# Seven block products instead of eight in the up projections of an encoder's last three FFNs

## The chip, the cores and the metric

The kernel runs on one core of one Trainium2 chip. The metric is the device time of one execution in microseconds (us); the figure given is the median of three runs. A profile is one execution, recorded by the hardware profiler.

In the texts PE is the matrix engine, PEld its loading of the stationary operand, DVE the vector engine, ACT the scalar engine, POOL a general engine, SP the engine that issues nearly all transfers (DMA). PE adds products up in PSUM banks, from which DVE and ACT read; everything else lies in SBUF.

## The reference

A trunk of two layers over 256 tokens of 1024 channels. Each layer is a feed-forward network (FFN), a mixing sub-layer and a second FFN, so the stages are FFN, mix, FFN, FFN, mix, FFN. What matters here is the FFN:

```python
def swiglu(h, w_up, w_down):
    a, b = jnp.split(h @ w_up, 2, axis=-1)
    return (jax.nn.silu(a) * b) @ w_down
...
        h = rms_norm(x, ffn1_pre_g[l])
        x = x + 0.5 * rms_norm(swiglu(h, ffn1_w_up[l], ffn1_w_down[l]), ffn1_post_g[l])
```

`w_up` is 1024 x 5632 (gate half, value half), `w_down` 2816 x 1024, all float32.

## The kernel before, in words

**Split operands.** A float32 product is made of three matmuls: each operand is a high part (rounded to the PE's reduced float32) and a low part (the rest), and high x high, high x low and low x high are added in one bank (`mm3`). ACT casts the high part, DVE subtracts it from the original for the low part (`split` for tokens and hidden values, `next_unit` for weights).

**Weights.** They come as units of 128 x 2048 (1 MB), laid out on the host in the order of use. SP loads them into `raw` tiles (pool `rawp`, three buffers); `next_unit` splits one into `wh` and `wl` (pool `wts`, five pairs of buffers), in two halves of 1024 columns, or in four quarters for the first five units of a stage. A buffer is loaded or split anew when its last reader is done.

**An FFN.** The 2816 hidden channels are 11 pairs of 128. For each pair the up projection needs two units (gate and value columns), the down projection one. Two pairs come first; then, for pair p from 2 to 10, the up projection of p and the down unit of p - 2 (`down`, `rows_chunk`: 24 matmuls into four banks `acc` that stay open for the whole FFN); the last three down units, first all token half 0 and then all token half 1, make the tail, which ends in `post_norm` and the next stage's `pre_norm`. Tokens are two halves c of 128; `xx` holds them transposed, high and low, as eight blocks of 128 channels.

**Two forms of the up projection.** The conventional one (`form_b2`; the first FFN throughout, pairs 0 and 1 elsewhere) keeps a token block stationary and moves 512 weight columns, 24 matmuls for each token half; `swiglu` makes the product with the gate, and two PE transposes a half (`turn`, kept in `pending` until a `flush`) bring it to the hidden tile `hid`. The other (`up2`, `form_a2`; pairs 2 to 10 of the last three FFNs) keeps the weights stationary and moves all tokens, 512 columns (high and low) for the high weight and 256 for the low one, so that its result is already transposed.

**What sets the order.** Each engine works through one queue in order. A scheduler orders the queues when the program is built, from the code's order and the buffers that are free; a wait in a queue holds up everything behind it. SP's transfers wait in its queue for their buffers. `ahead()`, called after pair 4, prepares the next mix in an FFN that comes ahead of one: in the fourth stage `mem_gain`, which loads the transposed memory tokens and splits them.

Of the kernel before, what the change touches and what calls it, by code (L numbers as in the profile page):

```python
# [17 lines left out]
P = 128  # L18
# [17 lines left out]
T_SC = (242, 336)  # L36
T_KT = (200, 222)
# [10 lines left out]
def encoder_kernel(ctx, tc, x_d, xt_d, mem_d, memt_d, pos_d, w_d, gains_d, cols_d, lamv_d, poolw_d, cst_d, out_d):  # L48
# [4 lines left out]
    rawp = ctx.enter_context(tc.tile_pool(name="rawp", bufs=3))  # L53
# [17 lines left out]
    def mb_bank():  # L71
        return mmp.tile([P, 512], F32, name="mb")
# [32 lines left out]
    def next_unit():  # L105
        parts = 4 if fine[0] > 0 else 2
        fine[0] -= 1
        if not raws:
            load_unit()
        raw = raws.pop(0)  # L110
        h = wts.tile([P, 2048], F32R, name="wh")
        l = wts.tile([P, 2048], F32R, name="wl")
        n = 2048 // parts
        for s in range(parts):
            cs = slice(s * n, (s + 1) * n)
            high = nc.scalar.copy(out=h[:, cs], in_=raw[:, cs])  # L116
            low = nc.vector.tensor_tensor(out=l[:, cs], in0=raw[:, cs], in1=h.bitcast(F32)[:, cs], op=ALU.subtract)  # L117
# [4 lines left out]
        return h, l  # L122

# [55 lines left out]
    def pre_norm(c, src, g, xx):  # L179
# [24 lines left out]
        return turn  # L204
# [81 lines left out]
    def ffn(i, xx, late, g_post, finish, ahead, raw_rstd=None):  # L286
# [4 lines left out]
        def hid_pair(p):  # L291
            hid[p] = (hids.tile([P, 2, 2, P], F32R, name="hid"), hids.tile([P, 2, 2, P], F32R, name="hid"))
            return hid[p]

        def lhs_of(c, kk, k):
            return hid[kk][0][:, c, k, :], hid[kk][1][:, c, k, :]

        def down(p):
# [7 lines left out]
        pending = []  # L306

        def flush():
            while pending:
                pending.pop(0)()  # L310
# [7 lines left out]

        def up_first(p, ws):
            banks = [ma_bank(), ma_bank()]  # L320
            for i, w in enumerate(ws):
                for c in range(2):
                    mm3(banks[c], half_b(w, i, c, xx), i == 0, i == 1)
            for c in range(2):
                swiglu(p, c, banks[c])

        def swiglu(p, c, ps):
            sg = t2((P, 2, P))
            gate, value = (ps[:, 256 * j:256 * j + 256].rearrange("p (u m) -> p u m", u=2) for j in range(2))
            hn = t2((P, 2, P))  # L330
            if raw_rstd:
                nc.scalar.activation(out=sg, in_=gate, func=AF.Silu, scale=raw_rstd[c])
                nc.vector.scalar_tensor_tensor(out=hn, in0=value, scalar=raw_rstd[c], in1=sg, op0=ALU.mult, op1=ALU.mult)
            else:
                nc.scalar.activation(out=sg, in_=gate, func=AF.Silu)
                nc.vector.tensor_tensor(out=hn, in0=value, in1=sg, op=ALU.mult)

            def turn():
                tp = mb_bank()
                for u in range(2):  # L340
                    nc.tensor.transpose(out=tp[:, u * P:(u + 1) * P], in_=hn[:, u, :], identity=ident)  # L341
                tv = tp[:, 0:256].rearrange("p (u t) -> p u t", u=2)
                split(tv, hid[p][0][:, c], hid[p][1][:, c])

            pending.append(turn)

        def up2(p, u):
            w = next_unit()
            banks = [ma_bank(), mb_bank()]
            for i in range(2):  # L350
                form_a2(banks[i], w, slice(i * P, (i + 1) * P), xx)
            flush()
            t = t2()
            for i in range(2):
                half = t[:, i * S:(i + 1) * S]
                nc.scalar.copy(out=half, in_=banks[i][:, S:2 * S])  # L356
                nc.vector.tensor_tensor(out=half, in0=banks[i][:, 0:S], in1=half, op=ALU.add)  # L357
            nc.scalar.activation(out=t[:, 0:S], in_=t[:, 0:S], func=AF.Silu)  # L358
            nc.vector.tensor_tensor(out=t[:, 0:S], in0=t[:, 0:S], in1=t[:, S:2 * S], op=ALU.mult)
            split(t[:, 0:S].rearrange("p (c t) -> p c t", c=2), hid[p][0][:, :, u, :], hid[p][1][:, :, u, :])  # L360

        ws = [(next_unit(), next_unit()) for _ in range(1 if raw_rstd else 2)]
        if raw_rstd:
            hs, ls = first_high, first_low
# [6 lines left out]
        for p in range(2):  # L371
            hid_pair(p)
        if raw_rstd:
# [3 lines left out]
        else:  # L377
            done = []
# [4 lines left out]
        for p in range(2, NPR):  # L383
            hid_pair(p)
            if raw_rstd:
                w2 = (next_unit(), next_unit())
                for c in range(2):
                    up(p, c, w2)
            else:
                for u in range(2):  # L390
                    up2(p, u)
            if p - 2 <= NPR - 4:
                down(p - 2)
            if p == 4:
                ahead()
        todo = [(next_unit(), p) for p in range(NPR - 3, NPR)]
# [125 lines left out]
    def mix(l, xx, late, mm, finish):  # L522
# [10 lines left out]
        vc = mixp.tile([P, 2, S], F32, name="vc")  # L533
        up = mixp.tile([P, 2, S + 16], F32, name="up")
        pooled = mixp.tile([P, 2, S], F32, name="pooled")
        pw = mixp.tile([P, 2, P], F32, name="pw")
# [261 lines left out]

    for i, (kind, l, row) in enumerate(stages):
        nx = {}  # L800

        def finish(c):
# [5 lines left out]
            if c == 0:  # L808
                nx["xx"] = xt_pair()
                nx["g"] = gain(stages[i + 1][1] * 10 + stages[i + 1][2])  # L810
            return pre_norm(c, halves(x[c]), nx["g"], nx["xx"])()

        if kind == "ffn":
# [7 lines left out]
            late = ffn(i, cur, late, gain(l * 10 + row + 1), finish, ahead, [rst[:, c:c + 1] for c in range(2)] if i == 0 else None)  # L821
        else:
            late = mix(l, cur, late, mem, finish)
        cur, mem = nx.get("xx"), nx.get("mem")
# [24 lines left out]
def _pack(a, np):  # L849
# [5 lines left out]

    def wide(w, idx):
        both = w[:, idx].reshape(2, 4, P, 512).transpose(0, 2, 1, 3)
        units.extend(np.ascontiguousarray(both[i]).reshape(P, 2048) for i in range(2))
# [4 lines left out]
    def ffn(up, down, first):  # L863
        for p in range(NPR):
            if p < 2 or first:
                wide(up, np.r_[256 * p:256 * p + 256, D_FF + 256 * p:D_FF + 256 * p + 256])
            else:
                for i in (2 * p, 2 * p + 1):
                    cols(up, np.r_[P * i:P * i + P, D_FF + P * i:D_FF + P * i + P])
            if 0 <= p - 2 <= NPR - 4:  # L870
                rows(down, p - 2)
# [61 lines left out]
```

## Time and profile before

| | |
|---|---|
| runs shown | 1138.71 us median (1138.63 to 1139.41) |
| the profiled execution's own time | 1138.92 us |
| its span, first to last instruction | 1136.9 us |
| busy: PE, DVE, ACT | 1127.8, 749.6, 626.8 us |
| one late FFN (third stage, 384.20 to 570.05 us) | 185.85 us, DVE busy 120.77 |
| one repeat in it, an up pair and a down unit | 16.72 us |
| bytes read from HBM | 216.33 MB, mean 191 GB/s |

The profiled execution's time is 0.2 us above the median; 2.0 us lie outside its span. Lines are named L and a number. In groups by line an entry reads: line, engine, operation, output tile <- input tiles, shapes, count | busy us, mean ns of one | idle us of the engine just before them and what ended it. A chain row is a start, a length and a piece. A matmul's duration includes its way through the array, so that two in a row overlap; the distance between starts is what one costs.

### The profile page before, as it was taken

To read this page: it belongs to the slowest core of one execution; us is meant where nothing else is said; L and a number is where in the kernel's file an instruction comes from. 1 tells how busy PE (TensorE), PEld (TensorE's weight loads), DVE (VectorE), ACT (ScalarE), POOL (GpSimd) and SP (SyncE) were. 2 spreads that over 40 slices of the span, in tenths; PEclk is the share of its full clock that TensorE was granted. 3 is DMA by queue.
4 is the path that set the end of the run, shared out by engine and by line. 5 is a ranking of instruction groups with operands and counts; after the bars stand their busy time and mean duration, and the time that the engine had idled before them with its cause. 6 is when DMAs were issued, how large, how long until landed. Compare 5 with 4: busy or idle time off the path is not lost.

```text
span 1136.9 us, 14731 instructions
## 1 busy us (share of the span) xinstructions
PE 1127.8 (99%) x5679; PEld 943.7 (83%) x5679; DVE 749.6 (66%) x1164; ACT 626.8 (55%) x1121; POOL 25.6 (2%) x37
## 2 busy tenths in 40 slices
PE   9999999999999999999999999999999999999997
PEld 6888888888788888888888888888887888888886
DVE  6767456567758866566586756575676688666553
ACT  7666445456573565555565655555566546555541
POOL 0000000000000100000000000010000001000000
PEclk9999999999999999999999999999999999999999
DMA  8976553544554575555465655545455545655530
GB/s 318 340 239 229 194 189 131 213 171 148 205 183 168 204 256 192 186 185 186 148 238 206 222 189 184 186 158 204 161 180 184 203 148 177 249 185 185 186 111 37
DMA packets 35493, 218.32 MB, mean 192 GB/s; under 512 B 4192, under 2 KB 4448, under 8 KB 11232
## 3 DMA queue, kind: packets, MB, share of 16 engines
q1 hardware_dynamic: 35424, 217.40, 53.4%
q8 instruction: 44, 0.72, 0.2%
q14 instruction: 25, 0.20, 0.1%
HBM read 216.33 MB, written 1.05 MB: 191 GB/s over the span
## 4 chain that ended last, share of the span: by engine, by line
PE 97%; DMA 1%; ACT 1%; DVE 0%; POOL 0%; issue 0%; SPq 0%; DVEq 0%; POOLq 0%; ACTq 0%
PE ma L224 36%; PE acc L266 25%; PE mb L243 13%; PE ma L243 13%; PE mb L224 2%; PE acc L224 2%; PE mb L199 1%; PE acc L599 1%; PE mb L341 1%; PE acc L622 1%; PE mb L497 1%; PE acc L685 1%; DMA hid<-in_xt 1%; DMA raw<-in_w 0%; PE acc L669 0%; PE mb L758 0%
## 5 line engine op out<-in xcount | busy, mean ns | idle before, releaser
L117 DVE TENSOR_TENSOR wl<-raw,wh 128x1024 fp32r<-128x1024 f32 (+1 forms) x444 | 459.0, 1075 | 150.8 <-ACT wh L116 145.0
L116 ACT CAST wh<-raw 128x1024 fp32r<-128x1024 f32 (+1 forms) x444 | 391.3, 935 | 187.8 <-issue 99.9
L224 PE MATMUL ma<-wh,xhl 128*128 128x512 f32 x1184 | 376.6, 393 | 0.8 <-ACT wh L116 0.8
L224 PEld LDWEIGHTS ma<-wh,xhl 128*128 128x128 f32 x1184 | 221.4, 188 | 47.5 <-ACT wh L116 1.7
L224 PE MATMUL ma<-wl,xhl 128*128 128x512 f32 x592 | 233.6, 395 | 0.2 <-DVE wl L117 0.2
L266 PE MATMUL acc<-wh,hid 128*128 128x512 f32 x704 | 224.6, 391 | 0.0
L243 PE MATMUL ma<-xhl,wh 128*128 128x512 f32 x432 | 157.4, 398 | 0.0
L243 PE MATMUL mb<-xhl,wh 128*128 128x512 f32 x432 | 157.0, 397 | 0.0
L266 PEld LDWEIGHTS acc<-wh,hid 128*128 128x128 f32 x704 | 132.2, 188 | 26.2
L266 PE MATMUL acc<-wl,hid 128*128 128x512 f32 x352 | 137.1, 389 | 0.0
L224 PEld LDWEIGHTS ma<-wl,xhl 128*128 128x128 f32 x592 | 111.3, 188 | 23.9 <-DVE wl L117 1.2
L243 PE MATMUL mb<-xhl,wl 128*128 128x256 f32 x432 | 112.5, 281 | 0.0
L243 PE MATMUL ma<-xhl,wl 128*128 128x256 f32 x432 | 112.4, 281 | 0.0
L243 PEld LDWEIGHTS ma<-xhl,wh 128*128 128x128 f32 x432 | 81.2, 188 | 15.8
L243 PEld LDWEIGHTS mb<-xhl,wh 128*128 128x128 f32 x432 | 81.5, 189 | 14.5
L357 DVE TENSOR_TENSOR s<-mb,s 128x256 f32<-128x256 f32 x54 | 22.9, 424 | 103.8 <-ACT s L356 103.8
L243 PEld LDWEIGHTS mb<-xhl,wl 128*128 128x128 f32 x432 | 81.6, 189 | 5.0
L243 PEld LDWEIGHTS ma<-xhl,wl 128*128 128x128 f32 x432 | 81.5, 189 | 4.6
L266 PEld LDWEIGHTS acc<-wl,hid 128*128 128x128 f32 x352 | 66.2, 188 | 13.7
L356 ACT COPY s<-mb 128x256 f32<-128x256 f32 x54 | 20.2, 373 | 58.7 <-PE mb L243 58.7
L358 ACT ACTIVATE s<-s 128x256 f32<-128x256 f32 x54 | 22.6, 418 | 50.6 <-DVE s L357 50.6
L140 POOL TENSOR_TENSOR sm<-sm,mhalf 128x1 f32<-128x1 f32 (+1 forms) x26 | 22.6, 869 | 1024.5 <-DVE sm L149 845.6
(162 smaller groups left out, 966.0 us busy)
## 6 DMA issues: line engine op xcount, KB each, us to landing
raw<-in_w SPq DMA_DIRECT2D x189, 1024.0 KB, 4.8
gain<-in_gains SPq DMA_DIRECT2D x17, 512.0 KB, 5.1
raw<-in_w SPq DMA_DIRECT2D x8, 256.0 KB, 5.7
hid<-in_memt SPq DMA_DIRECT2D x8, 256.0 KB, 6.0
hid<-in_xt SPq DMA_DIRECT2D x4, 256.0 KB, 5.6
raw<-in_w SPq DMA_DIRECT2D x2, 512.0 KB, 6.9
x<-in_x SPq DMA_DIRECT2D x4, 256.0 KB, 6.6
hid<-in_mem SPq DMA_DIRECT2D x4, 256.0 KB, 6.1
```

The costliest lines, as they stand in the source:

```text
L116: high = nc.scalar.copy(out=h[:, cs], in_=raw[:, cs])
L117: low = nc.vector.tensor_tensor(out=l[:, cs], in0=raw[:, cs], in1=h.bitcast(F32)[:, cs], op=ALU.subtract)
L140: nc.gpsimd.tensor_tensor(out=r, in0=v, in1=mhalf[:, :n], op=ALU.pow)
L199: tps.append(nc.tensor.transpose(out=ps[:, k * P:(k + 1) * P], in_=xn[:, i * P:(i + 1) * P], identity=ident))
L224: done.append(nc.tensor.matmul(out=out, lhsT=lhsT, rhs=rhs, start=(first and i == 0), stop=(last and i == n - 1)))
L243: nc.tensor.matmul(out=o, lhsT=ww[:, k, ms], rhs=rhs, start=(k == 0 and o is full), stop=(k == KT - 1 and o is full))
L266: done.append(nc.tensor.matmul(out=banks[b], lhsT=a, rhs=ww[:, k, fs], start=(kk == first and k == 0 and i == 0), stop=(kk == last and k = ...
L341: nc.tensor.transpose(out=tp[:, u * P:(u + 1) * P], in_=hn[:, u, :], identity=ident)
L356: nc.scalar.copy(out=half, in_=banks[i][:, S:2 * S])
L357: nc.vector.tensor_tensor(out=half, in0=banks[i][:, 0:S], in1=half, op=ALU.add)
L358: nc.scalar.activation(out=t[:, 0:S], in_=t[:, 0:S], func=AF.Silu)
L497: ins.append(nc.tensor.transpose(out=tp[:, i * P:(i + 1) * P], in_=a[:, hh, kt * P:(kt + 1) * P], identity=ident))
```

## The change

In the last three FFNs, pairs 2 to 10 are now three single pairs in the conventional form (2, 5, 8) and three groups of two pairs (3 and 4, 6 and 7, 9 and 10). A group's product is tokens (two halves of 128) x channels (two halves of 512) by channels x columns (512 gate columns of two pairs, 512 value columns of them): a 2 x 2 by 2 x 2 block product. It is computed with seven block products of 12 matmuls each (Winograd's form of Strassen's method) in place of eight.

For it the transposed tokens are also kept in float32 (`keep`, four copies by ACT in `pre_norm`), and `token_sums` makes four sums of them on DVE and splits these. For each group DVE makes four sums of raw weight units in place (`add` on 128 x 2048, line 364 of the new file), seven units are split instead of four (`split_unit`, line 120), and the seven results are combined by seven sums of 128 x 512 (also line 364) and two products with the gate (line 385). In `group` the products are, in order, a, d, b, c, e, f, g.

```diff
+PLAN = [[(t[0], int(t[1:])) for t in plan.split()] for plan in (
+    "u2 d0 u3 d1 u4 d2 u5 d3 u6 d4 u7 d5 u8 d6 u9 d7 u10",
+    "u2 d0 g3 d1 d2 u5 d3 g6 d4 d5 u8 d6 g9 d7",
+)]
...
-    rawp = ctx.enter_context(tc.tile_pool(name="rawp", bufs=3))
+    rawp = ctx.enter_context(tc.tile_pool(name="rawp", bufs=5))
...
-    mixp = ctx.enter_context(tc.tile_pool(name="mixp", bufs=1))
-    s2 = ctx.enter_context(tc.tile_pool(name="s2", bufs=5))
+    s2 = ctx.enter_context(tc.tile_pool(name="s2", bufs=8))
...
+                if keep is not None:
+                    keep[c, b] = t2()
+                    nc.scalar.copy(out=keep[c, b], in_=ps)
...
             for c in range(2):
                 rows_chunk(c, acc[c], [(w, p)], lhs_of, 0, NPR - 1)
+                flush(1 - c)
...
+        def token_sums():
+            a11, a12, a21, a22 = (kept[c, b] for c in range(2) for b in range(2))
+            s1 = t2()
+            nc.vector.tensor_tensor(out=s1, in0=a22, in1=a21, op=ALU.subtract)
+            nc.vector.tensor_tensor(out=a21, in0=a11, in1=a21, op=ALU.subtract)
+            nc.vector.scalar_tensor_tensor(out=a11, in0=s1, scalar=-1.0, in1=a11, op0=ALU.mult, op1=ALU.subtract)
+            nc.vector.scalar_tensor_tensor(out=a12, in0=a11, scalar=-1.0, in1=a12, op0=ALU.mult, op1=ALU.subtract)
+            for j, t in enumerate((s1, a11, a21, a12)):
+                split(t.rearrange("p (k t) -> p k t", t=P), sums[:, 0, 4 * j:4 * j + 4, :], sums[:, 1, 4 * j:4 * j + 4, :])
+
+        def group(p):
+            def turn(c, value, gate):
+                nc.scalar.activation(out=gate, in_=gate, func=AF.Silu)
+                nc.vector.scalar_tensor_tensor(out=value, in0=value, scalar=-1.0, in1=gate, op0=ALU.mult, op1=ALU.mult)
+                turned(value, c, [p, p + 1])
+
+            w11, w12, w22, w21 = (next_raw() for _ in range(4))
+            a = ma_bank()
+            product(a, tokens(0, 0), split_unit(w11, 2))
+            flush()
+            s = t2()
+            nc.scalar.copy(out=s, in_=a)
+            add(w11, w11, w12)
+            d = mb_bank()
+            product(d, summed(0), split_unit(w11, 2))
+            flush()
+            add(w11, w11, w22)
+            add(w12, w12, w22)
+            b = mb_bank()
+            product(b, summed(1), split_unit(w11, 2))
+            u2, u3 = t2(), t2()
+            add(u2, s, b)
+            c = ma_bank()
+            product(c, summed(2), split_unit(w12, 2))
+            add(u3, u2, c)
+            add(u2, u2, d)
+            e = ma_bank()
+            product(e, tokens(0, 1), split_unit(w21, 2))
+            add(s, s, e)
+            v1 = t2()
+            add(v1, u3, d)
+            add(w21, w21, w11)
+            g = ma_bank()
+            f = mb_bank()
+            product(f, summed(3), split_unit(w22, 2))
+            add(u2, u2, f)
+            turn(0, u2, s)
+            product(g, tokens(1, 1), split_unit(w21, 2))
+            add(u3, u3, g)
+            turn(1, v1, u3)
...
-        for p in range(2, NPR):
-            hid_pair(p)
-            if raw_rstd:
-                w2 = (next_unit(), next_unit())
-                for c in range(2):
-                    up(p, c, w2)
-            else:
-                for u in range(2):
-                    up2(p, u)
-            if p - 2 <= NPR - 4:
-                down(p - 2)
-            if p == 4:
+            token_sums()
+        for n, (what, p) in enumerate(PLAN[bool(kept)]):
+            if what == "d":
+                down(p)
+            elif what == "u":
+                up_both(p)
+            else:
+                group(p)
+            if not kept and n == 5:
                 ahead()
+        if kept:
+            ahead()
```

`turned` is the old `turn` for one or two pairs (two or four transposes); `up_both` is a conventional pair; `product` is `mm3` over four channel blocks. The host lays the units out in the order of `PLAN`. The mix's own tiles (`mixp` before) lie in one `raw` buffer.

Where the queues change: first PE, at the end of an up projection and the start of the next down unit, in the third stage. Before (`xhl` are the tokens, moving; `mb` the bank), the last matmuls of a unit:

```order
L243 MATMUL mb_3814<-xhl_3209,wh_3807 128x512
L243 MATMUL mb_3814<-xhl_3209,wl_3808 128x256
L243 MATMUL mb_3814<-xhl_3209,wh_3807 128x512
L243 MATMUL mb_3814<-xhl_3209,wl_3808 128x256
L243 MATMUL mb_3814<-xhl_3209,wh_3807 128x512
```

After, the last product of the second group (`ma_4147` is g; `wh_4170` and `wl_4171` are the split of w21 + w11) and the first matmuls of the down unit behind it (`wh_4193`), with the engines that each waits for:

```order
L235 MATMUL ma_4147<-wh_4170,xhl_3203 128x512 [waits DVE_49,Activation_49]
L235 MATMUL ma_4147<-wl_4171,xhl_3203 128x512 [waits DVE_49]
L235 MATMUL ma_4147<-wh_4170,xhl_3203 128x512 x2
L235 MATMUL ma_4147<-wl_4171,xhl_3203 128x512
L235 MATMUL ma_4147<-wh_4170,xhl_3203 128x512
L235 MATMUL ma_4147<-wh_4170,xhl_3203 128x512 [waits Activation_49]
L235 MATMUL ma_4147<-wl_4171,xhl_3203 128x512 [waits DVE_49]
L235 MATMUL ma_4147<-wh_4170,xhl_3203 128x512 x2
L235 MATMUL ma_4147<-wl_4171,xhl_3203 128x512
L235 MATMUL ma_4147<-wh_4170,xhl_3203 128x512
L277 MATMUL acc_3632<-wh_4193,hid_3855 128x512 [waits Activation_49]
L277 MATMUL acc_3632<-wl_4194,hid_3855 128x512 [waits DVE_49]
```

A unit of 32 matmuls in two widths has become products of 12 in one width, and each half of a split weight is waited for on its own.

The second place is DVE, in the same stage. Before, two unit splits of an up projection with the sums of a unit's result (`s2`) and the split of its hidden value between them:

```order
L117 TENSOR_TENSOR wl_3774<-raw_3771,wh_3773 128x1024 [waits DMAHW6_49,Activation_49]
L117 TENSOR_TENSOR wl_3774<-raw_3771,wh_3773 128x1024 [waits Activation_49]
L157 TENSOR_TENSOR hid_3519<-s2_3571,hid_3518 128x2x128 [waits Activation_49]
L357 TENSOR_TENSOR s2_3622<-ma_3588,s2_3622 128x256 [waits Activation_49]
L357 TENSOR_TENSOR s2_3622<-mb_3589,s2_3622 128x256 [waits Activation_49]
L359 TENSOR_TENSOR s2_3622<-s2_3622 128x256 [waits DVE_49]
L117 TENSOR_TENSOR wl_3808<-raw_3805,wh_3807 128x1024 [waits DMAHW7_49,Activation_49]
L117 TENSOR_TENSOR wl_3808<-raw_3805,wh_3807 128x1024 [waits Activation_49]
```

After, in the second group, from the second half of e's weight to the second half of g's (`wl_4150` is f's split, `wl_4171` g's; `s2_4100` is u2, `s2_4101` u3, `s2_4057` s, `s2_4144` v1):

```order
L120 TENSOR_TENSOR wl_4126<-raw_4036,wh_4125 128x1024 [waits Activation_49]
L120 TENSOR_TENSOR wl_4150<-raw_4034,wh_4149 128x1024 [waits PE_49,Activation_49]
L364 TENSOR_TENSOR raw_4036<-raw_4036,raw_4030 128x2048 [waits DVE_49]
L364 TENSOR_TENSOR s2_4100<-s2_4057,mb_4081 128x512 [waits PE_49]
L120 TENSOR_TENSOR wl_4150<-raw_4034,wh_4149 128x1024 [waits Activation_49]
L364 TENSOR_TENSOR s2_4101<-s2_4100,ma_4103 128x512 [waits DVE_49,PE_49]
L120 TENSOR_TENSOR wl_4171<-raw_4036,wh_4170 128x1024 [waits Activation_49]
L364 TENSOR_TENSOR s2_4100<-s2_4100,mb_4060 128x512 [waits DVE_49]
L364 TENSOR_TENSOR s2_4057<-s2_4057,ma_4124 128x512 [waits PE_49]
L364 TENSOR_TENSOR s2_4144<-s2_4101,mb_4060 128x512
L120 TENSOR_TENSOR wl_4171<-raw_4036,wh_4170 128x1024 [waits Activation_49]
```

Sums that wait for PE's products now stand in DVE's queue between the halves of the splits that PE's next products wait for.

The third place is DVE in the first group of the same stage, where the order of the same steps is another (`wl_3806` is g's split, `s2_3735` u2, `mb_3783` f, `s2_3692` s with the gate, `wl_3829` the next down unit's split, `s2_3736` u3, `ma_3782` g). Nothing stands there before: in its place were rows like those shown.

```order
L120 TENSOR_TENSOR wl_3806<-raw_3671,wh_3805 128x1024 [waits Activation_49]
L364 TENSOR_TENSOR s2_3735<-s2_3735,mb_3783 128x512 [waits DVE_49,PE_49]
L120 TENSOR_TENSOR wl_3806<-raw_3671,wh_3805 128x1024 [waits Activation_49]
L385 SCALAR_TENSOR_TENSOR s2_3735<-s2_3735,s2_3692 128x512 [waits DVE_49,Activation_49]
L120 TENSOR_TENSOR wl_3829<-raw_3826,wh_3828 128x1024 [waits DMAHW7_49]
L364 TENSOR_TENSOR s2_3736<-s2_3736,ma_3782 128x512 [waits PE_49]
L120 TENSOR_TENSOR wl_3829<-raw_3826,wh_3828 128x1024
```

Here the second half of g's weight is split only behind the sum that waits for f, and the down unit's second half behind the sum that waits for g.

More of the change, by code (lines that the diff above doesn't have):

```diff
@@ L317, in up, with up_both, product, tokens @@
             return now
+        def up_both(p):
+            ws = (next_unit(), next_unit())
+            for c in range(2):
+                up(p, c, ws)
+        def product(out, at, w, first=True, last=True):
+            wv = [t.rearrange("p (k m) -> p k m", k=4) for t in w]
+            return mm3(out, [(at(k), (wv[0][:, k, :], wv[1][:, k, :])) for k in range(4)], first, last)
+        def tokens(c, b):
+            return lambda k: (xx[0][:, c, 4 * b + k, :], xx[1][:, c, 4 * b + k, :])
+        def add(out, a, b):
+            nc.vector.tensor_tensor(out=out, in0=a, in1=b, op=ALU.add)
@@ L319, in up_first @@
         def up_first(p, ws):
             banks = [ma_bank(), ma_bank()]
-            for i, w in enumerate(ws):
+            for j, w in enumerate(ws):
                 for c in range(2):
-                    mm3(banks[c], half_b(w, i, c, xx), i == 0, i == 1)
+                    mm3(banks[c], half_b(w, j, c, xx), j == 0, j == 1)
             for c in range(2):
                 swiglu(p, c, banks[c])
[L327 to L330, printed above, removed]
-            if raw_rstd:
-                nc.scalar.activation(out=sg, in_=gate, func=AF.Silu, scale=raw_rstd[c])
-                nc.vector.scalar_tensor_tensor(out=hn, in0=value, scalar=raw_rstd[c], in1=sg, op0=ALU.mult, op1=ALU.mult)
-            else:
[L335 to L339, printed above, removed]
-                for u in range(2):
[L341 to L360, printed above, removed]
@@ L362, in ffn @@
-        ws = [(next_unit(), next_unit()) for _ in range(1 if raw_rstd else 2)]
         if raw_rstd:
+            ws = [(next_unit(), next_unit())]
             hs, ls = first_high, first_low
@@ L377, in ffn @@
         else:
+            ws = [(next_unit(), next_unit()) for _ in range(2)]
             done = []
@@ L819, in ahead @@
                     nx["mem"] = mem_gain(l)
-            late = ffn(i, cur, late, gain(l * 10 + row + 1), finish, ahead, [rst[:, c:c + 1] for c in range(2)] if i == 0 else None)
+            late = ffn(i, cur, late, kept, gain(l * 10 + row + 1), finish, ahead, [rst[:, c:c + 1] for c in range(2)] if i == 0 else None)
         else:
             late = mix(l, cur, late, mem, finish)
-        cur, mem = nx.get("xx"), nx.get("mem")
+        cur, mem, kept = nx.get("xx"), nx.get("mem"), nx.get("kept")
 def _constants(np):
@@ L854, in cols, with block @@
         units.append(np.ascontiguousarray(w[:, idx].reshape(KT, P, 256).transpose(1, 0, 2)).reshape(P, 2048))
+    def block(w, half, col):
+        units.append(np.ascontiguousarray(w[512 * half:512 * half + 512, col:col + 512].reshape(4, P, 512).transpose(1, 0, 2)).reshape(P, 2048))
     def wide(w, idx):
-        both = w[:, idx].reshape(2, 4, P, 512).transpose(0, 2, 1, 3)
-        units.extend(np.ascontiguousarray(both[i]).reshape(P, 2048) for i in range(2))
+        both = w[:, idx]
+        for half in range(2):
+            block(both, half, 0)
     def rows(w, j):
@@ L863, in ffn, with pair @@
     def ffn(up, down, first):
-        for p in range(NPR):
-            if p < 2 or first:
-                wide(up, np.r_[256 * p:256 * p + 256, D_FF + 256 * p:D_FF + 256 * p + 256])
-            else:
[L868 to L871, printed above, removed]
+        def pair(p):
+            wide(up, np.r_[256 * p:256 * p + 256, D_FF + 256 * p:D_FF + 256 * p + 256])
+        pair(0)
+        pair(1)
+        for what, p in PLAN[not first]:
+            if what == "d":
+                rows(down, p)
+            elif what == "u":
+                pair(p)
+            else:
+                for half, col in ((0, 0), (0, D_FF), (1, D_FF), (1, 0)):
+                    block(up, half, 256 * p + col)
         for p in range(NPR - 3, NPR):
```

67 lines of the change are left out of this document (43 added, 24 removed).

## The prediction

> **What bounds the kernel now.** I read the page's busy shares first, then who made the matrix engine (PE) wait, then the chain of waits through one repeat of the late feed-forward layers (FFNs), then the same stretch by engine.
>
> ```profile
> span 1136.9 us, 14731 instructions
> PE 1127.8 (99%) x5679; PEld 943.7 (83%) x5679; DVE 749.6 (66%) x1164; ACT 626.8 (55%) x1121; POOL 25.6 (2%) x37
> PE 97%; DMA 1%; ACT 1%; DVE 0%; POOL 0%; issue 0%; SPq 0%; DVEq 0%; POOLq 0%; ACTq 0%
> PE acc L796 <- DVE up L585: 1.2, 1, 1.2
> PE ma L224 <- ACT wh L116: 0.8, 1, 0.8
> ```
>
> PE is busy almost throughout, the chain that ended last is 97% PE, and the largest wait, 1.2 us, is at the kernel's start. So the time is the sum of what PE issues, and an edit pays only by shortening PE's list without making PE wait. Busy time is modelled; I cost PE by start-to-start times from the chain (start, length, piece). One repeat of a late FFN comes first (two units of one pair, then a down unit), then one of the first FFN, whose pairs have the conventional form.
>
> ```profile
> 424.51 2.81 PE ma L243 x16
> 427.32 2.82 PE mb L243 x16
> 430.14 2.82 PE ma L243 x16
> 432.96 2.82 PE mb L243 x16
> 435.78 5.45 PE acc L266 x24
> 441.23 0.93 PE ma L243 x5
> ...
> 47.91 5.44 PE ma L224 x24
> 53.36 0.22 PE mb L341 x2
> 53.58 5.48 PE ma L224 x24
> 59.05 0.22 PE mb L341 x2
> 59.27 5.47 PE acc L266 x24
> ```
>
> A late pair takes 435.78 - 424.51 = 11.27 us and its repeat 441.23 - 424.51 = 16.72. A conventional matmul of 512 columns takes 5.46/24 = 0.2275 us; a transpose takes 0.11.
>
> ```profile
> 384.20:570.05 185.85, 185.85 (x961) 158.20 (x961) 120.77 (x182) 101.53 (x179) 3.50 (x4) 1.00 0.56 198
> 424.51:441.23 16.72, 16.72 (x89) 14.31 (x89) 10.12 (x14) 8.72 (x14) 0.00 (x0) 1.00 0.53 186
> 384.20:407.58 23.38, 23.38 (x111) 19.36 (x111) 20.09 (x33) 14.92 (x29) 2.08 (x2) 1.00 0.81 275
> 553.00:570.05 17.05, 17.05 (x81) 14.20 (x80) 11.67 (x23) 9.67 (x24) 1.41 (x2) 1.00 0.32 118
> ```
>
> These are stretches: a whole late FFN, one repeat, the FFN's first two pairs, its tail. Behind a stretch stand its length, the busy us (and instructions) of PE, PEld, DVE, ACT and POOL, PE's granted clock, the DMA share and GB/s. DVE is idle for 65.1 us of the FFN and 6.6 us of a repeat. The clock is 1.00.
>
> **The change, part by part.** *PE's list.* Each of three late FFNs loses nine pairs: 9 x 11.27 = 101.4 us. It gains three conventional pairs, each 48 matmuls and four transposes: 48 x 0.2275 + 4 x 0.11 = 11.36, so 34.1. It gains three groups, each 7 x 12 = 84 matmuls and eight transposes: 19.11 + 0.88 = 19.99, so 60.0. Net 94.1 - 101.4 = -7.3 an FFN, -22.0 in all. All of it lies on the path.
>
> *DVE's list.* The group pays in vector work. The rows for it (busy, then mean ns of one) and how closely instructions follow one another:
>
> ```profile
> L117 DVE TENSOR_TENSOR wl<-raw,wh 128x1024 fp32r<-128x1024 f32 x324 | 383.0, 1220 | 139.9 <-ACT wh L116 134.3 <-issue 1.1 <-PE ma L224 0.4
> L723 DVE TENSOR_TENSOR hid<-ma,gain 128x512 f32<-128x512 f32 x24 | 16.4, 684 | 12.2 <-PE ma L224 12.0
> L216 DVE SCALAR_TENSOR_TENSOR x<-s,sm,x 128x512 f32<-128x512 f32 x24 | 16.9, 747 | 0.9
> L157 DVE TENSOR_TENSOR hid<-mb,hid 128x256 fp32r<-128x256 f32 x34 | 14.1, 414 | 1.8 <-ACT hid L156 1.7
> L116 ACT CAST wh<-raw 128x1024 fp32r<-128x1024 f32 x324 | 325.0, 1052 | 182.2 <-issue 99.9 <-PE ma L224 60.5 <-PE acc L266 12.2
> ...
> 453.89 2.36 DVE L117 TENSOR_TENSOR wl<-raw,wh 128x1024 fp32r<-128x1024 f32 x2
> 456.17 0.42 DVE L157 TENSOR_TENSOR hid<-s,hid 128x256 fp32r<-128x256 f32 x1
> ...
> 342.01 0.68 DVE L750 TENSOR_TENSOR hid<-mb,hid 128x512 f32<-128x512 f32 x1
> 342.73 0.69 DVE L752 TENSOR_TENSOR hid<-hid 128x512 f32<-128x512 f32 x1
> 343.35 0.69 DVE L750 TENSOR_TENSOR hid<-acc,hid 128x512 f32<-128x512 f32 x1
> ```
>
> Two halves of a split start at 453.89 and the next instruction at 456.17: 1.14 us each, 0.08 less than the duration. A sum that needs the one just before it starts 0.72 after it (342.01 to 342.73), an independent one 0.62 or less; L752, with both operands in SBUF, lasts as long as those with one in PSUM. The new sum of a whole raw unit, 128x2048, is in no row. From 512 to 1024 columns a tensor_tensor grows by 0.536 us, so two such steps more give 1.22 + 2 x 0.536 = 2.29, and 2.21 start to start. The nearest bounds are 1.22 (no row with fewer columns can be longer) and four of L752, 2.74; I take 2.21, as the three sizes lie on one line.
>
> Now a stretch that repeats, group, two downs, pair, down, on PE: 19.99 + 3 x 5.46 + 11.36 = 47.7 us, against 3 x 16.72 = 50.2 before. On DVE, start to start: 12 units split (7 + 3 + 2), 24 x 1.14 = 27.4; four raw sums, 8.8; seven result sums, 4.2 to 4.3; two products by the gate, 1.3; six splits of the hidden and two products of the pair, 2.7; some eight sums that follow their own operand, 1.0; one wait for ACT's cast of the third product's weight, which can begin only when the sum has ended (the cast's 1.05 and a hand-over), 1.15. Total 46.6. So DVE goes from 30.4 of 50.2 to 46.6 of 47.7: PE stays the bound, by 1.1 us in 47.7.
>
> That holds if DVE is far enough ahead when a group begins, since the group alone asks 32 us of DVE in PE's 20. Five pairs of split weights hold the lead. I followed DVE, ACT and PE through two groups with these prices. When PE starts the second group's first product, DVE is inside the split of the third; when PE needs the last product's second half, it has been ready for about 1 us, and the first down unit's second half comes within 0.3 us of its need. In the first group of each FFN the last product is tightest: counted from the end of the fifth product, its first half is ready after 2.6 us and the sixth product ends after 2.73; DVE then waits there for the sixth result, adds, and has the second half ready after 4.7, which PE (six matmuls, and four of the down unit issued between) needs after 5.0. No stall comes out, but margins of 0.3 to 1 us at three or four places of each group, with some ten hand-overs that no row prices. I put 0.5 us a group there: 9 x 0.5 = 4.5; the ends are 0 and rival B.
>
> *What lies beside other work, at nothing.* The rows for it: a weight unit's landing time, a copy like the four that are added at each entry, and a vector instruction of `ahead`:
>
> ```profile
> raw<-in_w SPq DMA_DIRECT2D x189, 1024.0 KB, 4.8
> L499 ACT COPY s<-mb 128x512 f32<-128x512 f32 x16 | 9.0, 586 | 8.3 <-PE mb L497 8.3
> L168 DVE SCALAR_TENSOR_TENSOR xhl<-hid,colt,xhl 128x256 fp32r<-128x256 f32 x16 | 6.6, 480 | 0.2 <-ACT xhl L167 0.2
> ```
>
> ACT: four extra copies of the transposed tokens at each entry (128x512, 0.59 us each) between two casts; PE has 11 matmuls (2.5 us) and then 12 on the other half before it needs the delayed one. Per stretch ACT has 24 casts of 1.05 us and about 5 us else (two gates, a copy, the hidden), 30 of 47.7. The token sums are 5 us of DVE before the second product; it has the 20 us of the third pair, a down unit and a product, with 11 us of other work. If that cover went, product two would wait. The weights' transfers keep their number and their one queue. A group holds four of the five raw buffers; the first comes free some 13 us before the group ends, the next at 9 and 7, and SP's next waits are for exactly these, so nothing late stands in front of an early load, and 4.8 us to land is within those leads. `ahead` in the fourth FFN moves behind the last group: four loads on SP, eight casts on ACT and eight vector instructions of 0.48, 3.9 us on DVE ahead of the closing norm. The tail's DVE idle time, 17.05 - 11.67 = 5.4 us, covers it; without that, the norm and PE's next tokens wait up to 3.9 once. In the first FFN only the transposes' place changes.
>
> Sum on the profiled execution: 1138.92 - 22.0 + 4.5 = 1121.4; the median of the runs, 1138.71, stands 0.2 lower: **1121**.
>
> **Rivals.** *B: DVE is the bound.* If each instruction costs its full duration, the stretch is 24 x 1.22 + 4 x 2.29 + 7 x 0.684 + 2 x 0.747 + 6 x 0.414 + 2 x 0.42 + 1.15 = 49.2 us, and each of nine groups loses 1.5 us against PE's 47.7: 1116.7 + 13.5 = 1130. The 0.08 us overlaps above speak against it; the unpriced hand-overs speak for something like it. The Trainium skill, "VectorE: DVE Perf Modes", section "The DRAIN you can't avoid", says that the next vector operation does not start until the pipe has emptied, and adds that one that is not held starts earlier; taken at its first half, it gives this rival, and the trace's 453.89 and 456.17 agree with its second.
> *C: slower.* The in-place sum of raw units (line 364 after) costs far more than the line through 256, 512 and 1024 says. DVE's stretch passes the old 50.2 us once each such sum takes 2.21 + (50.2 - 46.6)/4 = 3.1 us; at double my price, 4.4, it is 55.4, and 1138.9 + 9 x 5.2 = 1186. L752, in place in SBUF, shows no such surcharge.
> *D: the gain is whole, and more.* No stall at all, 1116.7, and the five raw buffers bring the start's fourth and fifth unit earlier. PE's first real matmul and the end of its second pair:
>
> ```profile
> 6.83 0.50 PE L224 MATMUL ma<-wh,xhl 128*128 128x512 f32 x1 [0.77 <-ACT wh L116]
> ...
> 31.04 5.50 PE ma L224 x24
> ```
>
> Between them lie 96 matmuls and six transposes, 22.5 us of 24.2, so up to 1.7 us waits there: 1115.
>
> **How the numbers follow.** A as summed, 0.60 (1117 to 1126); B, 0.25 (1126 to 1137); C, 0.07; D, 0.08. The range of 8 in 10 leaves out C, the upper part of B and part of D: 1116 to 1133. Beyond 0.2%, about what a measurement here can tell from no change (2.3 us, so below 1136.4): faster A, D and most of B, 0.90; same, B's end, 0.03; slower C, 0.07.
>
> **What would show it.** PE right: 84 matmuls of a group in 19.1 us and a late FFN's stretch near 180 us instead of 185.9. DVE right: starts 1.14 apart in splits, a 128x2048 sum of 2.29, and DVE busy over 95% of the 47.7 us stretch. Stalls: PE's waits on the low halves (the split line) in the low tens of us in all would be B; a few us, A. Wrong would be: PE waits inside a product well over 1 us, or a stretch above 50 us.

## The result, and the profile after

The changed kernel takes 1126.73 us (median of four runs, 1125.79 to 1127.05) against 1139.06 us before in the same series (1138.63 to 1139.44): a ratio of 0.9891, 95% interval 0.9873 to 0.9908. That is 12.3 us less; 17.7 were forecast. The profiled execution took 1127.05 us.

First the page's span, busy shares and chain; then PE's waits in full (total us, times, longest):

```profile
span 1124.9 us, 13897 instructions
PE 1109.0 (99%) x5247; PEld 913.2 (81%) x5247; DVE 893.5 (79%) x1215; ACT 651.9 (58%) x1082; POOL 26.1 (2%) x37
PE 92%; DVE 4%; ACT 1%; DMA 1%; POOL 1%; issue 0%; SPq 0%; DVEq 0%; POOLq 0%; ACTq 0%
```

```profile
PE mb L325 <- DVE s L341: 5.3, 3, 2.0
PE acc L860 <- DVE s L857: 1.2, 1, 1.2
PE ma L235 <- ACT wh L119: 1.1, 2, 0.9
PE mb L207 <- DVE s L199: 1.1, 1, 1.1
PE ma L235 <- DVE wl L120: 0.5, 2, 0.2
PE mb L703 <- DVE s L699: 0.4, 2, 0.2
```

PE waits 9.6 us where it waited 2.9, and the chain has fallen from 97% to 92% PE. Two rows are new: 5.3 us for DVE's product of the first pair (line 341) and 1.1 us for a closing norm (line 199). No wait stands inside a group. The groups are where forecast. Below are the stretch from one group to the next in the third stage and that whole stage, by engine; then the chain through the same stretch; then DVE's new sum of raw units and four halves of a split in a row.

```profile
475.44:523.18 47.74, 47.74 (x217) 39.43 (x217) 46.62 (x48) 29.41 (x37) 0.00 (x0) 1.00 0.55 198
384.91:565.71 180.80, 178.85 (x818) 147.59 (x817) 169.62 (x200) 110.23 (x165) 3.48 (x4) 1.00 0.57 204
```

```profile
475.44 2.77 PE ma L235 x12
478.21 5.44 PE mb L235 x24
483.65 5.44 PE ma L235 x24
489.09 2.72 PE mb L235 x12
491.81 2.72 PE ma L235 x12
494.53 2.72 PE acc L277 x12
...
523.18 0.92 PE ma L235 x4
```

```profile
L364 DVE TENSOR_TENSOR raw<-raw 128x2048 f32<-128x2048 f32 x36 | 82.4, 2288 | 0.4
```

```profile
504.84 4.63 DVE L120 TENSOR_TENSOR wl<-raw,wh 128x1024 fp32r<-128x1024 f32 x4
```

The seven products follow one another without a gap, the stretch takes 47.74 us with PE busy in all of it, and DVE is busy for 46.62. Of the 48 DVE instructions in that row 26 are halves of weight splits that start in it, where the stretch's own list has 24: DVE gets ahead by one unit here. A whole raw unit's sum takes 2.29 us. The stage takes 180.80 us instead of 185.85.

**Where the time went: the entry of a late FFN.** The next rows are ACT, DVE and PE at the third stage's entry (start, length, instruction; in brackets the idle time before it and what ended it):

```profile
393.94 1.07 ACT L164 CAST xhl<-mb 128x512 fp32r<-128x512 f32 x2 [1.56 <-PE mb L207]
396.55 1.18 ACT L212 COPY s<-mb 128x512 f32<-128x512 f32 x2 [1.53 <-DVE xhl L165]
397.63 0.67 ACT L340 ACTIVATE s<-ma 128x256 f32<-128x256 f32 x2
...
395.82 1.29 DVE L165 TENSOR_TENSOR xhl<-mb,xhl 128x512 fp32r<-128x512 f32 x2
398.22 0.76 DVE L341 TENSOR_TENSOR s<-ma,s 128x256 f32<-128x256 f32 x2
...
398.79 0.41 PE L325 MATMUL mb<-ident,s 128*128 128x128 f32 x2 [1.95 <-DVE s L341]
```

The SiLU of pair 0 (line 340) now stands in ACT's queue behind the casts of the late tokens and two of the four new copies (line 212). The copies wait for DVE's split of the same banks, so ACT is idle 1.53 us and the SiLU runs at 397.63. DVE's product follows at 398.22, and PE, whose queue has pair 0's transposes ahead of everything else, waits 1.95 us. Before, that SiLU stood ahead of the late casts:

```profile
389.77 0.38 ACT L335 ACTIVATE s<-ma 128x256 f32<-128x256 f32 x1
393.06 1.07 ACT L156 CAST xhl<-mb 128x512 fp32r<-128x512 f32 x2 [2.40 <-PE mb L199]
```

The same wait comes at the two other entries (1.41 and 1.99 us). Behind the last one PE's granted clock drops: first what follows the three waits, by stretch (the clock is the third figure from the end), then the 24 matmuls behind the last wait and the next 24.

```profile
398.80:402.00 3.20, 3.20 (x15) 2.68 (x16) 0.60 (x2) 0.37 (x1) 0.00 (x0) 1.00 1.00 353
580.00:585.00 5.00, 5.00 (x25) 4.09 (x23) 1.97 (x3) 2.01 (x2) 0.00 (x0) 1.00 0.49 198
950.90:955.00 4.10, 4.09 (x13) 3.24 (x14) 0.62 (x2) 0.37 (x1) 0.00 (x0) 0.60 0.74 260
```

```profile
951.32 7.07 PE ma L235 x24
958.61 5.45 PE ma L235 x24
```

At full clock the 24 behind an entry's transposes take 5.50 us (third stage), so 7.07 - 5.50 = 1.57 us are lost, at one entry of three. The fourth stage's tail has the other new wait: `memt` is loaded only behind the last group's transposes (line 325 in the chain), and the closing norm's squares (line 155) stand in ACT's queue behind its casts.

```profile
725.75 7.41 DMA hid<-in_memt
734.00 0.90 ACT xhl L175 x2
734.90 0.58 ACT junk L155 x2
744.47 1.06 PE mb L207 x8
```

Against 1138.92 - 22.0 = 1116.9 the profiled execution has 10.1 us more: 5.35 at the entries, 1.57 by the clock, 1.06 at this tail and 0.75 at the start and in the first FFN (PE's 31.60 against 31.04 at the third pair, and 0.02 a repeat). Counted from start to start, each of these four waits costs 0.16 us more than its idle time: the last matmul ahead of the third stage's wait starts at 396.46 and the transposes at 398.79, which is 2.33 us, less 0.23 for the matmul. That is 0.6 of the other 1.4 us; the rest I did not locate.

### The profile page after: what moved, and what is told of

Its sections match the earlier page's. It is cut to its first block, busy times and chain, and to the rows that moved or that the text cites. A ratio compares the mean times of both kernels' runs of the same rounds, so it can differ in the third digit from the quotient of the medians.

```text
span 1124.9 us, 13897 instructions
## 1 busy us (share of the span) xinstructions
PE 1109.0 (99%) x5247; PEld 913.2 (81%) x5247; DVE 893.5 (79%) x1215; ACT 651.9 (58%) x1082; POOL 26.1 (2%) x37
## 3 DMA queue, kind: packets, MB, share of 16 engines
HBM read 216.33 MB, written 1.05 MB: 193 GB/s over the span
## 4 chain that ended last, share of the span: by engine, by line
PE 92%; DVE 4%; ACT 1%; DMA 1%; POOL 1%; issue 0%; SPq 0%; DVEq 0%; POOLq 0%; ACTq 0%
PE ma L235 52%; PE acc L277 23%; PE mb L235 8%; DVE wl L120 2%; PE acc L235 2%; PE mb L325 2%; POOL sm L148 1%; PE acc L663 1%; DMA hid<-in_memt 1%; PE acc L686 1%; PE mb L563 1%; DVE x L227 1%; DMA raw<-in_w 1%; PE acc L749 1%; ACT wh L119 0%; PE mb L207 0%
## 5 line engine op out<-in xcount | busy, mean ns | idle before, releaser
L120 DVE TENSOR_TENSOR wl<-raw,wh 128x1024 fp32r<-128x1024 f32 (+1 forms) x498 | 524.2, 1092 | 101.6 <-ACT wh L119 99.0
L235 PE MATMUL ma<-wh,xhl 128*128 128x512 f32 x1760 | 562.3, 394 | 1.1 <-ACT wh L119 1.1
L119 ACT CAST wh<-raw 128x1024 fp32r<-128x1024 f32 (+1 forms) x498 | 445.0, 948 | 197.9 <-PE ma L235 65.6
L235 PEld LDWEIGHTS ma<-wh,xhl 128*128 128x128 f32 x1760 | 330.3, 188 | 70.8 <-ACT wh L119 2.4
L235 PE MATMUL ma<-wl,xhl 128*128 128x512 f32 x880 | 346.3, 394 | 0.5 <-DVE wl L120 0.5
L235 PEld LDWEIGHTS ma<-wl,xhl 128*128 128x128 f32 x880 | 165.8, 188 | 35.0 <-DVE wl L120 1.5
L235 PE MATMUL mb<-wh,xhl 128*128 128x512 f32 x280 | 90.5, 389 | 0.0
L364 DVE TENSOR_TENSOR raw<-raw 128x2048 f32<-128x2048 f32 x36 | 82.4, 2288 | 0.4
L235 PEld LDWEIGHTS mb<-wh,xhl 128*128 128x128 f32 x280 | 52.6, 188 | 11.0
L235 PE MATMUL mb<-wl,xhl 128*128 128x512 f32 x140 | 54.5, 389 | 0.0
```

Of the source, the lines that this page charges most:

```text
L235: done.append(nc.tensor.matmul(out=out, lhsT=lhsT, rhs=rhs, start=(first and i == 0), stop=(last and i == n - 1)))
L364: nc.vector.tensor_tensor(out=out, in0=a, in1=b, op=ALU.add)
```

## The experiments

The ratios go by the runs of the kernel before in the same series; a difference in us is one of medians. e1 to e4 ran on one chip, e5 to e8 on a second and e9 on a third, where the kernel before took 1139.47, 1138.96 and 1139.09 us, so a difference between these three is good to some 0.5 us. Theory "order": the missing gain is the SiLU's place behind the copies, with what the clock adds, and the memory's casts ahead of the norm. Its rival: DVE, busy 46.6 of 47.7 us, is already the bound, and the entries only show its lag.

| kernel | median, us (runs) | ratio to before, 95% |
|---|---|---|
| after | 1126.73 (4) | 0.9891, 0.9873 to 0.9908 |
| e1_own_buffer | 1120.23 (4) | 0.9830, 0.9818 to 0.9843 |
| e2_mem_early | 1128.04 (4) | 0.9893, 0.9879 to 0.9907 |
| e3_no_copies | 1119.18 (4) | 0.9821, 0.9809 to 0.9834 |
| e4_dve_plus2 | 1145.19 (6) | 1.0053, 1.0040 to 1.0067 |
| e5_own_buffer_dve_plus1 | 1126.58 (4) | 0.9883, 0.9866 to 0.9899 |
| e6_own_buffer_two_groups | 1127.92 (4) | 0.9898, 0.9883 to 0.9913 |
| e7_own_buffer_mem_early | 1119.33 (4) | 0.9823, 0.9808 to 0.9837 |
| e8_own_buffer_mem_in_mix | 1118.43 (4) | 0.9815, 0.9801 to 0.9830 |
| e9_mem_in_mix_warm14 | 1118.56 (5) | 0.9818, 0.9804 to 0.9831 |

**Another pool for two buffers (e1).**

```diff
-            sg, hn = t2((P, S)), t2((P, S))
+            sg, hn = [hids.tile([P, S], F32, name="hid") for _ in range(2)] if kept and p + c == 0 else (t2((P, S)), t2((P, S)))
```

> One line: the SiLU and the product of a late FFN's first pair (tokens 0) take their two buffers from the pool of the hidden, not from the pool in which the four copies of the tokens lie; so the SiLU may stand in ACT's queue ahead of the late tokens' casts and copies. Theory 'order' (the gain is missing because that SiLU stands behind the copies at each of three entries: PE waits 5.3 us in all, and the granted clock falls once behind such a wait, 1.6 us): 1126.7 - 5.3 - 1.6 = 1119.8, range 1118.8 to 1122 (the copies still hold the turning banks, which may leave some tenths at an entry). Rival 'DVE is the bound' (DVE is 46.6 us busy in 47.7, the waits at the entries are only where its lag comes to light): the waits turn up elsewhere, 1125.5 to 1127.

Measured 1120.23, 6.5 us less than the changed kernel. At the same entry ACT now has

```profile
391.06 0.37 ACT L340 ACTIVATE hid<-ma 128x256 f32<-128x256 f32 x1
394.27 1.07 ACT L164 CAST xhl<-mb 128x512 fp32r<-128x512 f32 x2 [1.28 <-PE mb L207]
396.61 1.18 ACT L212 COPY s<-mb 128x512 f32<-128x512 f32 x2 [1.26 <-DVE xhl L165]
397.25 0.44 PE L325 MATMUL mb<-ident,hid 128*128 128x128 f32 x2
```

The line names only a pool, yet the SiLU stands ahead of the casts. That a pool's buffers are given out in the order of the code, and so the SiLU's after the copies', is my reading; shown is that the pool alone moves it. The row of 5.3 us is gone from PE's waits and so is the fall of the clock at 950 us (in this execution it fell at the kernel's start instead, to 0.60 from 8 to 12 us). The theory holds, the rival falls: DVE's list is unchanged.

**Without the copies (e3).** The sums of the token blocks are formed from the high halves of the split tokens, and `nc.scalar.copy(out=keep[c, b], in_=ps)` goes.

> The four copies of the transposed tokens at each late FFN's entry are left out; the sums of token blocks are formed from the high halves of the split tokens alone (the low halves are left out of these sums). DVE's work keeps its number. Theory 'order': nothing stands between the SiLU and its bank, so as in the run with own buffers or up to 0.5 us an entry less: 1118.3 to 1120. Rival 'the copies' own time' (1.2 us of ACT that wait for DVE at each entry): this run gains and the run with own buffers does not. Rival 'DVE is the bound': 1125.5 to 1127, as DVE's list is as long.

Measured 1119.18, 1.05 us under e1; the intervals overlap. The direction agrees with e1's rows, in which the first copy ends near 397.2 and the transposes, which the trace shows waiting for it, start at 397.25. From a late FFN's start to its first group the three traced stretches take 121.27 us together without the copies and 121.82 in e1. So the copies cost some 0.2 us an entry by themselves, and 6.5 us by their place in the order.

**DVE's room (e4, e5).** The first half of a group's first low part is computed three times (e4, on the changed kernel) or twice (e5, on e1):

```diff
-            low = nc.vector.tensor_tensor(out=l[:, cs], in0=raw[:, cs], in1=h.bitcast(F32)[:, cs], op=ALU.subtract)
+            low = [nc.vector.tensor_tensor(out=l[:, cs], in0=raw[:, cs], in1=h.bitcast(F32)[:, cs], op=ALU.subtract) for _ in range(1 if s else 1 + more)][-1]
...
-            product(a, tokens(0, 0), split_unit(w11, 2))
+            product(a, tokens(0, 0), split_unit(w11, 2, 2))
```

> Two more vector instructions in each of the nine groups: the first half of the first weight unit's low part is computed three times instead of once (128x1024, 1.14 us each, the same result), so DVE's list grows by 2.28 us a group. Theory 'DVE is close to the bound but not it' (46.62 us busy of 47.74 in the second stretch of an FFN, 45.73 of 47.75 in the first, 39.84 of 42.52 in the last): the first loses 0.3, the second 1.2, the last nothing or what comes too late inside the group, so 1.5 to 3.5 us an FFN: 1131 to 1137. Rival 'DVE is already the bound': each group loses all 2.28, 20.5 in all, 1147. Rival 'there is more room than the busy time says': under 1.5 us in all, 1126.5 to 1128.

> On the kernel with own buffers (1120.2): one more vector instruction of 1.14 us in each of the nine groups (the first half of the first unit's low part is computed twice, the same result). Two of them a group cost 18.5 us where 20.5 were added. Theory 'a little room' (DVE busy 46.6 of 47.7 us in the second stretch, 45.7 in the first, 39.8 of 42.5 in the last): one instruction a group just fills the room, 0 to 0.5 us a group, 1120 to 1124. Rival 'no room, each vector instruction of a group is on the path': 9 x 1.14 = 10.3, 1130.5. Anything above that would be a fall of the granted clock behind new waits.

e4 took 18.5 us more than the changed kernel, for 20.5 us of added DVE work; e5 6.35 more than e1, for 10.3. Both lie above the first theory's range and below the rival's figure. The chain of e4 shows how, here inside its first group:

```profile
436.74 2.73 PE ma L235 x12
...
439.50 0.69 DVE s L364
440.18 2.20 DVE raw L364
442.39 1.79 DVE s L364 x3
444.18 1.15 DVE wl L120
...
445.37 2.79 PE mb L235 x11
```

PE now ends a product and waits for DVE's sums. In e4 PE's waits add up to 18.5 us instead of 9.6, and the clock falls behind three of them:

```profile
400.00:404.00 4.00, 4.00 (x14) 3.14 (x13) 0.09 (x1) 1.17 (x2) 0.00 (x0) 0.70 0.56 211
764.00:768.00 4.00, 4.00 (x12) 3.12 (x11) 3.82 (x7) 0.00 (x0) 0.00 (x0) 0.57 0.73 238
1008.00:1012.00 4.00, 2.89 (x8) 2.30 (x9) 4.00 (x4) 4.00 (x6) 0.00 (x0) 0.74 0.74 258
```

The two profiled executions, 1143.48 and 1127.05 us, lie 16.4 us apart. Of these, 8.9 are direct waits, inside the 4.5 to 10.5 that the theory made of them, and the clock adds 3.4: two falls more, each 1.72 us by (1 - clock) x length, as 0.43 x 4 at 764 us. The rest is PE busy for longer, which these rows do not divide.

Neither loss is spread evenly over the nine groups. The next rows are the third stage's first and second group, each from its first matmul to the one behind its 84, in e1 and then in e5:

```profile
425.94:445.09 19.15, 19.15 (x88) 15.85 (x85) 18.35 (x20) 15.24 (x19) 0.00 (x0) 1.00 0.46 164
473.70:492.87 19.17, 19.17 (x87) 15.85 (x86) 18.85 (x21) 15.49 (x19) 0.00 (x0) 1.00 0.56 191
425.97:445.66 19.69, 19.56 (x87) 15.65 (x86) 18.56 (x20) 16.16 (x19) 0.00 (x0) 1.00 0.41 135
474.35:493.48 19.13, 19.13 (x87) 15.87 (x86) 18.36 (x20) 15.21 (x18) 0.00 (x0) 1.00 0.46 165
```

One instruction more costs the first group 0.54 us and the second nothing. It is the same in the other late FFNs: e5's first groups take 19.69, 19.69 and 19.72 us, the six others 19.13. e4's two instructions cost the third stage's first group 3.0 us (22.19) and the two others 0.1 each (19.26 and 19.25). Most of e5's loss lies elsewhere. Of the 8.4 us between the profiled executions of e5 and e1, 5.3 come between the start of the fourth stage and that of the sixth, and only 0.7 of these up to the end of the last group. Behind it the order of the queues is another than in e1: one weight unit less is loaded ahead of the memory's tokens, that unit lands only at 736.85 us, and PE waits at the start of the mix, with the clock at 0.57 from 756 to 760 us.

```profile
728.24 8.61 DMA raw<-in_w
755.22 0.50 PE L235 MATMUL ma<-wl,xhl 128*128 128x512 f32 x1 [2.05 <-DVE wl L120]
```

So e5 does not give the room of each group. What the traces give is this: without an added instruction DVE is not the bound (e1). In the first group of a late FFN it comes within one instruction of it, and in the two others it has room for one and nearly for two. What the added instructions change at the fourth stage's end was not tested by itself.

**One group less (e6, on e1).** `"... u8 d6 g9 d7"` becomes `"... u8 d6 u9 d7 u10"`.

> On the kernel with own buffers (1120.2): the third group of each late FFN is replaced by two conventional pairs (g9 by u9 and u10, a down unit between), two groups instead of three. Theory 'PE's list': a group is 84 matmuls and eight transposes, 19.99 us, two pairs 22.72; three times 2.73 are 8.2: 1128.4, range 1127.5 to 1129.5. Rival 'the groups carry waits of their own': less is lost, with 0.5 us a group 6.7, 1126.9; with DVE as the bound in the last group still less.

Measured 7.7 us more than e1, against 8.2 by PE's list: a group is worth some 2.6 us of the 2.73. In the traces the third stage grows by 2.85 us (178.94 to 181.79) and the sixth, up to its last matmul, by 2.81, so no wait of the groups' own is seen.

**The memory's tokens (e2, e7, e8).** e2 loads them ahead of group 9 and leaves their casts where they were; e7 is e2 with e1's line; e8, also with that line, makes the casts in the mix:

```diff
-                group(p)
+                group(p, ahead(load=True) if p == 9 else None)
...
+        mm = mm((part, rope)) if callable(mm) else mm
```

> In the fourth FFN the four loads of the memory's tokens are issued ahead of the last group instead of behind it; their casts keep their place behind the group's turned hidden. Theory 'order': the closing norm no longer stands in ACT's queue behind a transfer of 7.4 us, and PE's one wait of 1.06 us before the next tokens' transposes goes: 1126.7 - 1.1 = 1125.6, range 1125.2 to 1126.2. Rival: eight casts and eight vector instructions (3.9 us of DVE) in that place are themselves the delay, and the wait stays: 1126.4 to 1127.

> Own buffers and the early loads of the memory's tokens together. The early loads took the wait at the fourth FFN's end from 1.06 to 0.4 us, but the run as a whole was no faster, because the granted clock fell behind two of the three entry waits instead of one. Theory 'the waits and the clock': with the entry waits gone the 0.7 us show: 1119.5, range 1118.7 to 1120.2. Rival 'the early loads cost elsewhere': 1120.2 to 1121.5.

> Own buffers, the memory's tokens loaded ahead of the fourth FFN's last group, and their eight casts and eight vector instructions (3.9 us of DVE) moved from that FFN's tail into the mix that follows, behind its second rotary step. Theory 'the norm was late because of them': PE's wait at that FFN's end goes wholly (1.1 to 1.3 us in the run with own buffers): 1119.0, range 1118.3 to 1119.6. Rival 'DVE has no 3.9 us to give there either': the mix's weights come late, 1119.6 to 1123.

e2's wait at the fourth stage's end fell from 1.1 to 0.4 us, and still its median was 1.3 us higher than the changed kernel's (equal by the ratios): in the profiled execution the clock fell behind two entry waits instead of one.

```profile
400.00:404.00 4.00, 4.00 (x13) 3.15 (x12) 0.00 (x0) 0.61 (x1) 0.00 (x0) 0.64 0.58 240
952.00:956.00 4.00, 4.00 (x13) 3.17 (x13) 0.47 (x2) 0.37 (x1) 0.00 (x0) 0.57 0.75 262
```

With the entry waits gone the steps come out as expected: 1119.33 (e7) and 1118.43 (e8), though each lies inside the interval of the one before, and e1 ran on another chip. That the wait is gone in e8 is seen in its chain, in which PE runs through that tail:

```profile
725.82 14.31 PE acc L277 x63
740.13 0.88 PE mb L207 x8
```

e8 is the best version run: 8.3 us under the changed kernel, 1.7 above 1138.7 - 22.0.

**The start (e9, on e8).** `WARM = 11` becomes 14.

> On the kernel with own buffers and the memory's gains in the mix (1118.4): 14 dummy matmuls at the start instead of 11, so that PE does not wait for 0.8 to 2.0 us between the last of them and the first real one. Theory 'the clock falls behind a PE wait': in three profiles the start's wait was 1.4 to 2.0 us and the granted clock of 8 to 12 us was 0.57 to 0.60 (some 1.6 us lost), in four with a wait of 0.8 to 0.9 us it was 1.00; without the wait the clock of that stretch stays 1.00 and the median falls by 0.5 to 1.6: 1116.8 to 1117.9. Rival 'the dummies themselves are late': three of them take up to 1.3 us, end after the first weights are there and push everything: 1118.6 to 1119.5, with the clock at 1.00 all the same.

PE's wait ahead of the first real matmul went, and the clock of 8 to 12 us was 1.00 instead of e8's 0.59. But the median stayed (1118.56), so the forecast of 1116.8 to 1117.9 failed. In the traces e9 has the transposes ahead of the third pair at 30.57 us where e8 has them at 31.33, and then a third stage that is 0.39 us longer; why the runs as a whole are no faster is not shown. One count in the expectation was off as well: in e2 and e7 the first real matmul takes 0.80 and 0.79 us, where it takes 0.49 to 0.51 in the other traces, though the clock's column reads 1.00 there. The column does not show every slow stretch.

## Why the prediction was right or wrong

- *PE's list, -22.0 us*: right. The stretch is 47.74 us against 47.7 forecast, and e6 confirms a group's worth from the other side.
- *DVE's list, 46.6 of 47.7*: the prices were right, the sum agrees by luck. The sum of a raw unit is right to the hundredth (2.29), and rival C (a dear sum) is excluded by that row. But the 46.6 holds a wait of 1.15 us, which is not busy time, and the measured 46.62 holds two halves more than the list; without them, 2 x 1.14, it is 44.3. So DVE had more room than forecast, as e4 and e5 show in all but the first group of an FFN. Rival B put the time at 1130 by DVE's full durations; four halves in 4.63 us show the overlaps, and no group waits.
- *Stalls in the groups, +4.5 us*: wrong, measured 0. The margins of 0.3 to 1 us held: e5's 1.14 us cost the first group 0.54, so its margin was some 0.6. It lies at the sixth product, not at the last, which the prediction named as the tightest.
- *The four copies at an entry, at nothing*: the step that failed. I costed the copies' 0.59 us against PE's next matmuls, and took for granted that they stand between the two casts. But PE's queue has pair 0's transposes right behind the 11 matmuls that I counted as cover, in the trace before too (at 395.81 us), and I did not ask what is queued behind them on ACT: pair 0's SiLU, with DVE's product and PE's transposes behind that. Measured 5.35 us of waits, 1.57 by the clock, 6.5 in e1.
- *`ahead` at the tail, at nothing or at most 3.9 us once*: the event came, at 1.06 us. The DVE work that I named as the price is not all of it; a transfer of 7.4 us that starts late stands ahead of the norm on ACT.
- *Five raw buffers bring the start forward (rival D)*: no. The third pair starts 0.56 us later here; the transposes ahead of it lie between 30.57 and 31.73 us in the profiles of this study, so this is within the start's scatter.

The total lay in the range because a term that was not there (4.5 us) stood in for part of the losses that were (10.1 us, 9.3 of them placed): 1121 forecast, 1126.7 measured, with the groups right and the entries missed.

## What to carry to other kernels

A small instruction is not free because its engine is half idle: look at what stands behind it in that engine's queue, and who waits for that. A buffer pool is also an order: here one line that names another pool moved an instruction ahead of four casts and copies. When the bound engine loses 2 us in one piece, count its clock too, and judge other edits only once such waits are gone, or the clock's chance hides them. An added instruction tells the room of the bound engine only at the places that grew: compare the traces stretch by stretch before dividing its cost by their number.

## What the runs showed of the hardware

PE's granted clock fell behind some single waits of about 2 us. In the middle of the kernels there are eight of 1.9 to 2.1 us, two in the changed kernel, two in e2, three in e4 and one in e5. Behind six of them the clock fell; it stayed at 1.00 behind the changed kernel's 1.95 us near 397 and behind e4's 1.96 us near 962. At the same entry near 397 it fell to 0.64 (400 to 404 us) behind e2's 1.94. e4 also has two close waits of 1.2 and 1.3 us at three places, and the clock fell behind one of these. The entry waits of 1.4 us (after, e2) were not followed by a fall, but at the kernel's start waits of 1.4 and 1.5 us were (e8, e5: 0.59 and 0.57 from 8 to 12 us). One fall cost 1.57 us where it could be read off the chain.

The Trainium skill, "TensorE: Matmul & The Clock Gate", part 1, "The HAM clock gate", has the clock halve after an idle window of about 3.4 us that runs freely; a free window would explain that equal waits differ, but the waits here are shorter than the window, so the measurement decides that 2 us can be enough.
